# Four of the first layer's six input chunks multiplied as two Strassen units, with chained weight sums

## The chip, the cores and the metric

The kernel runs on one core of one Trainium2 chip. The metric is device time in microseconds (us) for one execution of the whole program. The kernel before takes 2197.44 us, the median of 3 runs (2197.28 to 2199.9).

## The reference, cut to what matters

Two transformer-like layers work on x of 256 rows (tokens) by 2048 columns, in float32. The first layer, with the parts that the change touches:

```
h  = x @ ev_w_in                      # 256x2048 @ 2048x3072
za = gelu(h[:, :2048]); xb = h[:, 2048:]
u, v = split(za)                      # 1024 columns each
v  = layer_norm(v, g, b)
ya = u * (tril(w_s) @ v per head + b_s)        # "gate": mixes rows, 8 heads of 128
yb = (pooling of xb over windows 2,4,8,16) @ w_pool * scale
mix = concat(ya, yb) @ ev_w_out       # 256x2048 @ 2048x2048
x  = layer_norm(ALPHA*x + mix)
x  = layer_norm(ALPHA*x + conv_ffn(x))         # w_up 2048x11264, w_down 5632x2048
```

The second layer has a gated recurrent mixer (w_in 2048x8192, w_out 2048x2048) in place of the gate and the pooling, and a conv_ffn of its own.

## The kernel before, in words

Nearly all of the work is products of x (256 rows, two halves t0 and t1 of 128) with weights. A weight matrix is cut into tiles of 512 rows by 512 columns (1 MiB). Four such tiles on top of each other make a chunk of 512 output columns. A float32 product is made of three passes: each weight tile is split by ScalarE into a rounded part wh (line 178) and by VectorE into the remainder wl (line 181), x likewise into xh and xl, and TensorE adds up xh*wh + xh*wl + xl*wh. One weight tile is therefore 4 (slices of 128 rows) x 3 (passes) x 2 (row halves) = 24 matmuls of 128 columns by 512.

The class Weights runs this stream. `_load` lists the tiles to fetch, `_feed` lists the tiles to split, in the order of use. `take` hands out the next split tile; before that it splits up to two tiles ahead, and `more` issues the loads for which a buffer is free (three raw buffers for ordinary tiles of kind 0; one buffer per tag for those of kind 1). Loads are issued by SyncE. `std` lists ordinary tiles. `chain` lists a Strassen unit: two chunks of columns by seven block products. A Strassen product needs half of the matmuls of an ordinary tile (12: one row half alone), so the unit has 7 x 12 for the upper two tiles of both chunks, and 4 x 24 for the lower two. Three of its products use sums of weight tiles. These are built in two raw buffers a and b: a is loaded, a second tile is added to it by an accumulating transfer that GpSimd issues (line 110, `then`); after a's first use a third tile is added, and after a difference on VectorE (line 113) a fourth. `strassen` (line 399) runs the products on TensorE in the order of UNIT_R[0] (P1, P7, s, P3, s, P6, P2, P5, s, P4, s; s is an ordinary tile); `snap` (line 424) copies a product from its accumulator bank, and VectorE joins them. `combine` (line 373) builds the four sums of x blocks that the products need. The second layer's mixer uses all of this already; the first layer before the change does not: its six input chunks (columns 2, 3 for v, 4, 5 for xb, 0, 1 for u) all go through `chunk` (line 330), 4 tiles of 24 matmuls each.

Around the chunks: after chunk 2 the function `loads0` issues the constants on SyncE (the norm's g and b, w_s, biases, scale, identity, pooling bands, 2.5 MB in all), after chunk 3 v is normalized. `later(n, fn)` keeps a piece of work back until TensorE has been given n more tiles' worth of work (`tick`); the gate, the pooling and the transposes of u are given to it. In the kernel before, the gate runs inside chunk 5 and the pooling inside chunk 0. x itself (two halves of 1 MiB) is loaded on SyncE after chunk 3 into x_t and first read at the end of `out_proj`'s first chunk. The program is handed to a scheduler that orders each engine's instructions by their place in the program and by when it expects them to be ready; semaphores are set by it.

Of the kernel before, what the change touches and what calls it, by code (L numbers as in the profile page):

```python
# [9 lines left out]
F32 = mybir.dt.float32  # L10
# [8 lines left out]
P = 128  # L19
# [16 lines left out]
class Weights:  # L36
# [3 lines left out]
    def __init__(self, nc, raw, hl, ahead):  # L40
# [10 lines left out]

        self.extra = {}


    def _load(self, ap, tag):
        r = {"ap": ap, "tag": tag, "last": None, "tile": None, "then": None, "phase": self.phase}
        self.loads[tag != "w"].append(r)
        return r

# [38 lines left out]
                if ap is not None:  # L98
                    self.std([ap])

    def chain(self, aps, rest, others=()):


        nc = self.nc
        a, b = self._load(aps[3], "qa"), self._load(aps[2], "qb")
        unit = UNIT_R[len(others)]
        rest, others = iter(rest), iter(others)

        def add(ap):
            nc.gpsimd.dma_start(a["tile"].rearrange("p k n -> p (k n)"), ap, accum_op=ALU.add)  # L110

        def t1():
            nc.vector.tensor_tensor(out=b["tile"], in0=a["tile"], in1=b["tile"], op=ALU.subtract)
            add(aps[1])

        a["then"] = lambda: add(aps[2])
        products = {"P7": (a, (), None, lambda: add(aps[0])), "P3": (b,), "P6": (a, (b,), None, t1),
                    "P5": (b,), "P4": (a,)}
        plain = {"P1": aps[0], "P2": aps[1]}
        for f in unit:  # L120
            if f in products:
                self._feed(*products[f])
            else:
                ap = plain[f] if f in plain else next(rest if f == "s" else others, None)
                if ap is not None:
                    self.std([ap])


    def load(self, pieces=1, between=None, kind=0):
        r = self.loads[kind][self.n_load[kind]]  # L130
        tag = r["tag"]
        r["tile"] = w = self.raw[kind].tile([P, 4, 512], F32, name=f"w{kind}_{self.n_load[kind]}", tag=tag)
        n = 4 // pieces
        for k in range(0, 4, n):
            if between is not None:
                between(k)
            self.nc.sync.dma_start(w[:, k:k + n].rearrange("p k n -> p (k n)"),
                                   r["ap"][:, k * 512:(k + n) * 512])
        if r["then"]:
            r["then"]()  # L140
        self.ring.setdefault(tag, []).append(r)
        self.n_load[kind] += 1
# [60 lines left out]
def block_kernel(ctx: ExitStack, tc: tile.TileContext, a, out):  # L203
# [14 lines left out]
    aux = ctx.enter_context(tc.tile_pool(name="aux", bufs=4, space=PSUM))  # L218

    W = Weights(nc, raw, hl, 2)  # L220
    for c in (2, 3, 4, 5, 0, 1):
        W.std([a["w_ev_in"][c, g] for g in range(4)])
    for c in range(4):
        W.std([a["w_ev_out"][c, g] for g in (2, 3, 0, 1)])

# [44 lines left out]
    def new_T(kind, g, pool=acts):  # L270
        h = pool.tile([P, 4, S], F32R, name=f"{kind}h{g}", tag=f"{kind}h{g}")
        l = pool.tile([P, 4, S], F32R, name=f"{kind}l{g}", tag=f"{kind}l{g}")
        return h, l
# [13 lines left out]
    with tc.tile_pool(name="xload", bufs=2) as xl:  # L287
# [18 lines left out]
        for g in (2, 3):  # L306
            split(XT[g], xr[g], np.s_[:, :, :])
            W.cast(4)
    x_t = [resid.tile([P, D], F32, name=f"x{t}", tag=f"x{t}") for t in range(2)]


    waiting = []
# [197 lines left out]
    def normalize(dst, src, mean, rs, g, b):  # L510
        V.scalar_tensor_tensor(out=dst, in0=src, scalar=mean, in1=g, op0=ALU.subtract, op1=ALU.mult)  # L511
        V.scalar_tensor_tensor(out=dst, in0=dst, scalar=rs, in1=b, op0=ALU.mult, op1=ALU.add)  # L512
# [8 lines left out]
    def load_gb(g_ap, b_ap, n=D, eng=G):  # L521
        g = gbp.tile([P, D], F32, name="g", tag="g")
        b = gbp.tile([P, D], F32, name="b", tag="b")
        eng.dma_start(g[:, 0:n], g_ap.rearrange("(o n) -> o n", o=1).broadcast_to([P, n]))
        eng.dma_start(b[:, 0:n], b_ap.rearrange("(o n) -> o n", o=1).broadcast_to([P, n]))
        return g, b
# [135 lines left out]

    ymix = ExitStack()
    yp = ymix.enter_context(tc.tile_pool(name="ymix0", bufs=1))
    YT = [new_T("y", g, yp) for g in range(4)]
    with tc.tile_pool(name="work0", bufs=1) as wk:
        v_t = [wk.tile([P, 1024], F32, name=f"v{t}") for t in range(2)]
        b_t = [wk.tile([P, 1024], F32, name=f"xb{t}") for t in range(2)]
        ws = wk.tile([P, 8, P], F32, name="ws")
        bs = wk.tile([P, 8], F32, name="bs")  # L670
        psc = wk.tile([P, 8], F32, name="psc")
        band = wk.tile([P, 4, 384], F32, name="band")

        def loads0():
            gb = load_gb(a["ln_v_g"], a["ln_v_b"], 1024, nc.sync)
            nc.sync.dma_start(ws, a["w_sT"].rearrange("p (h t) -> p h t", h=8))
            nc.sync.dma_start(bs, a["b_sT"])
            nc.sync.dma_start(psc, a["pool_scT"])
            nc.sync.dma_start(cst, a["cst"][:, 0:384].rearrange("p (k n) -> p k n", k=3))
            nc.sync.dma_start(band, a["cst"][:, 512:2048].rearrange("p (w n) -> p w n", w=4))  # L680
            for h in range(8):
                G.affine_select(ws[:, h], ws[:, h], pattern=[[1, P]], compare_op=ALU.is_ge, fill=0.0,
                                base=0, channel_multiplier=-1)
            return gb

        stv = [wk.tile([P, 2, 6], F32, name=f"stv{t}") for t in range(2)]

        def after_v(c):
            def f(t, ps):
                vs = v_t[t][:, c * 512:(c + 1) * 512]  # L690
                A.activation(vs, ps, AF.Gelu_apprx_tanh)
                V.bn_stats(stv[t][:, c], vs)
                if c == 1:
                    mean, rs = moments(stv[t])
                    normalize(v_t[t], v_t[t], mean, rs, gv[:, 0:1024], bv[:, 0:1024])
            return f

        def gate(t):
            for q in range(2):
# [4 lines left out]
                for k in range(4):  # L704
                    h = 4 * q + k
                    A.activation(v_t[t][:, h * P:(h + 1) * P], pg[:, k], AF.Identity, bias=bs[:, h:h + 1])

        def after_b(c):
            def f(t, ps):
                A.activation(b_t[t][:, c * 512:(c + 1) * 512], ps, AF.Copy)  # L710
            return f

        def pool(gi):
            wp = wk.tile([P, 2, S], F32, name="wp", bufs=2)
# [13 lines left out]
                kb = (gi % 2) * 2 + d  # L728
                split(YT[2 + gi // 2], py[:, d], np.s_[:, kb, :], scale=psc[:, gi * 2 + d:gi * 2 + d + 1])

        def after_u(c):
            def f(t, ps):
                u = wk.tile([P, 512], F32, name="u", bufs=2)
                A.activation(u, ps, AF.Gelu_apprx_tanh)
                V.tensor_tensor(out=u, in0=u, in1=v_t[t][:, c * 512:(c + 1) * 512], op=ALU.mult)
                later(1, lambda: transpose_split(YT[c], u, t))
            return f

        chunk(XT, 4, after_v(0))
        gv, bv = loads0()  # L740
        chunk(XT, 4, after_v(1))
        lower_bound()
        for t in range(2):
            nc.sync.dma_start(x_t[t], a["x"][t * P:(t + 1) * P])
        chunk(XT, 4, after_b(0))
        later(1, lambda: gate(0))
        later(2, lambda: gate(1))
        chunk(XT, 4, after_b(1))
        for gi in range(4):
            later(1 + gi, lambda gi=gi: pool(gi))  # L750
        chunk(XT, 4, after_u(0))
        chunk(XT, 4, after_u(1))
        XT = out_proj([YT[g] for g in (2, 3, 0, 1)], 4, True, a["ln1_g"][0], a["ln1_b"][0])
    ymix.close()


# [356 lines left out]
```

## Time and profile before

| | us |
|---|---|
| median of 3 runs | 2197.44 |
| the profiled execution | 2202.97 |
| its span (first to last instruction) | 2201.2 |
| TensorE busy in it | 2157.1 (98%) |
| VectorE busy | 1767.4 (80%) |
| ScalarE busy | 1230.3 (56%) |
| DMA moved | 489.00 MB, mean 222 GB/s |

A row of the timeline has start, duration, engine, source line, operation and tiles. Matmuls overlap, so a matmul's own duration (0.39 us) is longer than the step from one to the next. "idle before" and an arrow tell how long the engine stood still and what released it. Windows give busy time by engine, the granted TensorE clock, the DMA engines' busy share and their rate. In the profile "w<-in_w_ev_in" is the load of a first-layer input tile, "POOLq" a transfer issued by GpSimd.

### The profile page before, as it was taken

The numbers are of one execution on the slowest core, as the hardware profiler recorded it, in microseconds if no ns is written. First come the engines' busy times: TensorE is split into PE (matmuls) and PEld (weight loads), VectorE is DVE, ScalarE is ACT, GpSimd is POOL, SyncE is SP. The second block draws the span as 40 slices with busy tenths as digits, with TensorE's granted clock in tenths as the row PEclk, the third lists the DMA queues.
The fourth block names the chain that finished last, engine by engine and source line by source line (L and its number), as shares of the span: only waits on it lengthen the run. The fifth ranks groups of instructions, "written<-read, shape, count | busy, mean of one in ns | idle before, by whom it ended". The sixth has DMA issues, their size and how long they took to land. (4 is left out here: it accounts for less than half of the span.)

```text
span 2201.2 us, 24814 instructions
## 1 busy us (share of the span) xinstructions
PE 2157.1 (98%) x9887; PEld 1779.9 (81%) x9887; DVE 1767.4 (80%) x1706; ACT 1230.3 (56%) x1150; POOL 125.8 (6%) x140
## 2 busy tenths in 40 slices
PE   9999999999999999989999999999999999999997
PEld 7888788888888888878778888778888888888886
DVE  5545888888888888897687887888888888888888
ACT  5443455555655555646575756636555655555662
POOL 1000200000000000020000000030000000000000
PEclk9999999999999999999999999999999999999999
DMA  8646476777667677537778687746777666677743
GB/s 324 268 151 234 152 243 222 236 247 239 215 217 226 219 241 248 184 128 259 222 236 252 220 256 229 232 173 204 234 243 238 218 223 213 227 241 240 242 150 141
DMA packets 71796, 489.00 MB, mean 222 GB/s; under 512 B 8465, under 2 KB 9121, under 8 KB 13953
## 3 DMA queue, kind: packets, MB, share of 16 engines
q1 hardware_dynamic: 60656, 411.56, 50.0%
q0 software_dynamic: 11024, 75.86, 17.1%
q8 instruction: 77, 1.26, 0.2%
q14 instruction: 39, 0.31, 0.0%
HBM read 443.34 MB, written 2.11 MB: 202 GB/s over the span
## 5 line engine op out<-in xcount | busy, mean ns | idle before, releaser
L181 DVE TENSOR_TENSOR wl<-w,wh 128x2048 fp32r<-128x2048 f32 (+1 forms) x471 | 1051.2, 2235 | 337.7 <-ACT wh L178 334.2
L178 ACT ACTIVATE wh<-w 128x2048 fp32r<-128x2048 f32 (+1 forms) x495 | 894.7, 1813 | 628.7 <-PE pd L566 262.2
L412 PE MATMUL ps<-wh,xh 128*128 128x512 f32 x1188 | 468.0, 394 | 0.0
L412 PE MATMUL ps<-wl,xh 128*128 128x512 f32 x1188 | 462.8, 390 | 1.1 <-DVE wl L181 1.1
L412 PE MATMUL ps<-wh,xl 128*128 128x512 f32 x1188 | 462.8, 390 | 0.0
L566 PE MATMUL pd<-wh,yh 128*128 128x512 f32 x736 | 287.2, 390 | 3.2 <-DVE x L574 3.2
L566 PE MATMUL pd<-wl,yh 128*128 128x512 f32 x736 | 286.5, 389 | 0.4 <-DVE wl L181 0.4
L566 PE MATMUL pd<-wh,yl 128*128 128x512 f32 x736 | 286.4, 390 | 0.5 <-DVE yl L280 0.4
L412 PEld LDWEIGHTS ps<-wh,xl 128*128 128x128 f32 x1188 | 223.0, 188 | 46.7
L412 PEld LDWEIGHTS ps<-wl,xh 128*128 128x128 f32 x1188 | 223.3, 188 | 46.2 <-DVE wl L181 1.9
L412 PEld LDWEIGHTS ps<-wh,xh 128*128 128x128 f32 x1188 | 223.1, 188 | 45.0 <-ACT wh L178 0.4
L412 PE MATMUL ps<-wh,sh 128*128 128x512 f32 x432 | 169.8, 393 | 0.8 <-ACT u L424 0.5
L412 PE MATMUL ps<-wl,sh 128*128 128x512 f32 x432 | 168.9, 391 | 1.1 <-DVE wl L181 1.1
L412 PE MATMUL ps<-wh,sl 128*128 128x512 f32 x432 | 168.7, 390 | 0.0
L566 PEld LDWEIGHTS pd<-wh,yh 128*128 128x128 f32 x736 | 138.2, 188 | 32.5 <-DVE x L574 4.0
L566 PEld LDWEIGHTS pd<-wh,yl 128*128 128x128 f32 x736 | 138.1, 188 | 30.3 <-DVE yl L280 1.6
L566 PEld LDWEIGHTS pd<-wl,yh 128*128 128x128 f32 x736 | 138.2, 188 | 29.3 <-DVE wl L181 0.8
L341 PE MATMUL ps<-wh,xh 128*128 128x512 f32 x384 | 151.8, 397 | 1.6 <-ACT wh L178 1.6
L341 PE MATMUL ps<-wl,xh 128*128 128x512 f32 x384 | 151.2, 394 | 0.3 <-DVE wl L181 0.3
L341 PE MATMUL ps<-wh,xl 128*128 128x512 f32 x384 | 150.8, 393 | 0.0
L789 DVE SCALAR_TENSOR_TENSOR hc<-ph,cw,hc 128x254 f32<-128x254 f32 (+1 forms) x352 | 145.8, 475 | 1.4 <-ACT hc L786 1.2
L786 ACT ACTIVATE hc<-ph,cw 128x256 f32<-128x256 f32 x176 | 89.1, 556 | 62.5 <-DVE hc L789 58.8
(223 smaller groups left out, 2216.5 us busy)
## 6 DMA issues: line engine op xcount, KB each, us to landing
w<-in_w_up SPq DMA_DIRECT2D x176, 1024.0 KB, 4.9
w<-in_w_down SPq DMA_DIRECT2D x88, 1024.0 KB, 4.9
w<-in_w_od_in SPq DMA_DIRECT2D x64, 1024.0 KB, 6.6
w<-w POOLq DMA_DIRECT2D x40, 1024.0 KB, 8.1
w<-in_w_od_in POOLq DMA_DIRECT2D x21, 1024.0 KB, 9.2
w<-in_w_ev_in SPq DMA_DIRECT2D x20, 1024.0 KB, 5.2
w<-in_w_ev_out SPq DMA_DIRECT2D x16, 1024.0 KB, 4.8
w<-in_w_od_out SPq DMA_DIRECT2D x16, 1024.0 KB, 7.2
```

Of the source, the lines that this page charges most:

```text
L178: self.nc.scalar.activation(h[:, sl], w[:, sl], AF.Copy)
L181: eng.tensor_tensor(out=l[:, sl], in0=w[:, sl], in1=h[:, sl].bitcast(F32), op=ALU.subtract)
L341: T.matmul(ps[t], s[:, k, ts], m[:, k], start=(gi == 0 and k == 0 and i == 0), stop=(gi == n - 1 and k == 3 and i == 2))
L412: T.matmul(bank_, x[:, k, ts], m[:, k], start=(id(bank_) not in started), stop=(k == 3 and i == 2), skip_group_check=True)
L566: T.matmul(ps, x[:, k, t * P:(t + 1) * P], m[:, k], start=(k == 0 and i == 0), stop=(k == 3 and i == 2))
L786: A.activation(ob, pt[:, k], AF.Identity, scale=cw[:, 2, blk:blk + 1], bias=cw[:, 3, blk:blk + 1])
L789: V.scalar_tensor_tensor(out=ob[:, s:S], in0=pt[:, k, 0:S - s], scalar=cw[:, w, blk:blk + 1], in1=ob[:, s:S], op0=ALU.mult, op1=ALU.add)
```

## The change

Chunks 4, 5 and chunks 0, 1 become two Strassen units. The x sums are built with `combine` between chunk 2 and chunk 3, in the two buffers g and b that held the norm's scale and shift (these move to a tile of the pool ymix0). The chain's buffers qa and qb lie in the same pool, in the space of YT (the transposed gate and pooling results), which is now allocated when a unit is done with them. The second unit's buffer a is the tile x_t[0], so x is loaded only after the second unit. `W.open += 1; W.more()` stands ahead of `loads0`: it issues at once every load of kind 1 whose buffer is free. The gate is now given to `later` ahead of the first unit, the pooling ahead of the second; gelu on u reads the unit's results in x_t[1].

```diff
--- before.py
+++ after.py
@@ -51,9 +51,11 @@
 
         self.extra = {}
 
+        self.home = {}
+
 
     def _load(self, ap, tag):
-        r = {"ap": ap, "tag": tag, "last": None, "tile": None, "then": None, "phase": self.phase}
+        r = {"ap": ap, "tag": tag, "last": None, "tile": self.home.get(tag), "then": None, "phase": self.phase}
         self.loads[tag != "w"].append(r)
         return r
 
@@ -98,11 +100,11 @@
                 if ap is not None:
                     self.std([ap])
 
-    def chain(self, aps, rest, others=()):
+    def chain(self, aps, rest, others=(), tag="qa"):
 
 
         nc = self.nc
-        a, b = self._load(aps[3], "qa"), self._load(aps[2], "qb")
+        a, b = self._load(aps[3], tag), self._load(aps[2], "qb")
         unit = UNIT_R[len(others)]
         rest, others = iter(rest), iter(others)
 
@@ -129,7 +131,9 @@
     def load(self, pieces=1, between=None, kind=0):
         r = self.loads[kind][self.n_load[kind]]
         tag = r["tag"]
-        r["tile"] = w = self.raw[kind].tile([P, 4, 512], F32, name=f"w{kind}_{self.n_load[kind]}", tag=tag)
+        if r["tile"] is None:
+            r["tile"] = self.raw[kind].tile([P, 4, 512], F32, name=f"w{kind}_{self.n_load[kind]}", tag=tag)
+        w = r["tile"]
         n = 4 // pieces
         for k in range(0, 4, n):
             if between is not None:
@@ -218,8 +222,15 @@
     aux = ctx.enter_context(tc.tile_pool(name="aux", bufs=4, space=PSUM))
 
     W = Weights(nc, raw, hl, 2)
-    for c in (2, 3, 4, 5, 0, 1):
-        W.std([a["w_ev_in"][c, g] for g in range(4)])
+    x_t = [resid.tile([P, D], F32, name=f"x{t}", tag=f"x{t}") for t in range(2)]
+    W.home["x0"] = x_t[0].rearrange("p (k n) -> p k n", k=4)
+    we = a["w_ev_in"]
+    for c in (2, 3):
+        W.std([we[c, g] for g in range(4)])
+    W.phase += 1
+    for c in (4, 0):
+        W.chain([we[c, 0], we[c, 1], we[c + 1, 1], we[c + 1, 0]],
+                [we[c, 2], we[c, 3], we[c + 1, 2], we[c + 1, 3]], tag="x0" if c == 0 else "qa")
     for c in range(4):
         W.std([a["w_ev_out"][c, g] for g in (2, 3, 0, 1)])
 
@@ -306,7 +317,6 @@
         for g in (2, 3):
             split(XT[g], xr[g], np.s_[:, :, :])
             W.cast(4)
-    x_t = [resid.tile([P, D], F32, name=f"x{t}", tag=f"x{t}") for t in range(2)]
 
 
     waiting = []
@@ -662,17 +672,25 @@
 
     ymix = ExitStack()
     yp = ymix.enter_context(tc.tile_pool(name="ymix0", bufs=1))
-    YT = [new_T("y", g, yp) for g in range(4)]
+    raw[1] = yp
+    YT = {}
+
+    def new_Y(g):
+
+        y = yp.tile([P, 2, 4, S], F32R, name=f"y{g}", tag=("qa", "qb", "qc", "qd")[g])
+        YT[g] = (y[:, 0], y[:, 1])
+
     with tc.tile_pool(name="work0", bufs=1) as wk:
         v_t = [wk.tile([P, 1024], F32, name=f"v{t}") for t in range(2)]
-        b_t = [wk.tile([P, 1024], F32, name=f"xb{t}") for t in range(2)]
         ws = wk.tile([P, 8, P], F32, name="ws")
         bs = wk.tile([P, 8], F32, name="bs")
         psc = wk.tile([P, 8], F32, name="psc")
         band = wk.tile([P, 4, 384], F32, name="band")
 
         def loads0():
-            gb = load_gb(a["ln_v_g"], a["ln_v_b"], 1024, nc.sync)
+            gb = yp.tile([P, 2, 1024], F32, name="gbv", tag="qc")
+            for i, ap in enumerate((a["ln_v_g"], a["ln_v_b"])):
+                nc.sync.dma_start(gb[:, i], ap.rearrange("(o n) -> o n", o=1).broadcast_to([P, 1024]))
             nc.sync.dma_start(ws, a["w_sT"].rearrange("p (h t) -> p h t", h=8))
             nc.sync.dma_start(bs, a["b_sT"])
             nc.sync.dma_start(psc, a["pool_scT"])
@@ -681,7 +699,7 @@
             for h in range(8):
                 G.affine_select(ws[:, h], ws[:, h], pattern=[[1, P]], compare_op=ALU.is_ge, fill=0.0,
                                 base=0, channel_multiplier=-1)
-            return gb
+            return gb[:, 0], gb[:, 1]
 
         stv = [wk.tile([P, 2, 6], F32, name=f"stv{t}") for t in range(2)]
 
@@ -692,7 +710,7 @@
                 V.bn_stats(stv[t][:, c], vs)
                 if c == 1:
                     mean, rs = moments(stv[t])
-                    normalize(v_t[t], v_t[t], mean, rs, gv[:, 0:1024], bv[:, 0:1024])
+                    normalize(v_t[t], v_t[t], mean, rs, gv, bv)
             return f
 
         def gate(t):
@@ -704,11 +722,6 @@
                 for k in range(4):
                     h = 4 * q + k
                     A.activation(v_t[t][:, h * P:(h + 1) * P], pg[:, k], AF.Identity, bias=bs[:, h:h + 1])
-
-        def after_b(c):
-            def f(t, ps):
-                A.activation(b_t[t][:, c * 512:(c + 1) * 512], ps, AF.Copy)
-            return f
 
         def pool(gi):
             wp = wk.tile([P, 2, S], F32, name="wp", bufs=2)
@@ -728,29 +741,51 @@
                 kb = (gi % 2) * 2 + d
                 split(YT[2 + gi // 2], py[:, d], np.s_[:, kb, :], scale=psc[:, gi * 2 + d:gi * 2 + d + 1])
 
-        def after_u(c):
-            def f(t, ps):
+        def done_u(c, tiles):
+            if c == 0:
+
+                new_Y(0)
+                new_Y(1)
+            for t in range(2):
                 u = wk.tile([P, 512], F32, name="u", bufs=2)
-                A.activation(u, ps, AF.Gelu_apprx_tanh)
+                A.activation(u, tiles[t], AF.Gelu_apprx_tanh)
                 V.tensor_tensor(out=u, in0=u, in1=v_t[t][:, c * 512:(c + 1) * 512], op=ALU.mult)
-                later(1, lambda: transpose_split(YT[c], u, t))
-            return f
+
+                later(0.5, lambda t=t, u=u: transpose_split(YT[c], u, t))
+
 
         chunk(XT, 4, after_v(0))
+        W.open += 1
+        W.more()
         gv, bv = loads0()
+        tmp = [wk.tile([P, 2, 4, P], F32, name=f"cmb{t}", tag=f"xb{t}") for t in range(2)]
+        XS = combine(XT, *(v[:, i] for v in tmp for i in range(2)))
         chunk(XT, 4, after_v(1))
+        b_t = [wk.tile([P, 1024], F32, name=f"xb{t}", tag=f"xb{t}") for t in range(2)]
         lower_bound()
+
+
+        def tile_b(name, tag=None):
+            t, c = {"p1": (0, 0), "u3": (1, 0), "z": (0, 1), "c22": (1, 1), "p17": (0, None)}[name]
+            return x_t[1][:, 0:512] if c is None else b_t[t][:, c * 512:(c + 1) * 512]
+
+        def tile_u(name, tag=None):
+            i = ("p1", "u3", "z", "c22", "p17").index(name)
+            return x_t[1][:, i * 512:(i + 1) * 512] if i < 4 else spare[:, 0:512]
+
+        later(1, lambda: gate(0))
+        later(2, lambda: gate(1))
+        strassen(XT, XS, tile_b, lambda c, tiles: None, (), UNIT_R[0])
+        new_Y(2)
+        new_Y(3)
+        spare = yp.tile([P, 4 * 512], F32, name="spare", tag="qa")
+        for gi in range(4):
+            later(1 + gi, lambda gi=gi: pool(gi))
+        strassen(XT, XS, tile_u, done_u, (), UNIT_R[0])
         for t in range(2):
             nc.sync.dma_start(x_t[t], a["x"][t * P:(t + 1) * P])
-        chunk(XT, 4, after_b(0))
-        later(1, lambda: gate(0))
-        later(2, lambda: gate(1))
-        chunk(XT, 4, after_b(1))
-        for gi in range(4):
-            later(1 + gi, lambda gi=gi: pool(gi))
-        chunk(XT, 4, after_u(0))
-        chunk(XT, 4, after_u(1))
         XT = out_proj([YT[g] for g in (2, 3, 0, 1)], 4, True, a["ln1_g"][0], a["ln1_b"][0])
+    del raw[1]
     ymix.close()
 
 
```

## Rows read from the trace of the kernel before

**Rows 1.** The profile's page: busy time of the engines, granted clock in 40 slices.
```profile
PE 2157.1 (98%) x9887; PEld 1779.9 (81%) x9887; DVE 1767.4 (80%) x1706; ACT 1230.3 (56%) x1150; POOL 125.8 (6%) x140
PEclk9999999999999999999999999999999999999999
```

**Rows 2.** Waits of TensorE from 0 to 260 us: total us, times, longest.
```profile
PE pt L493 <- DVE x L512: 4.6, 3, 2.7
PE ps L341 <- ACT wh L178: 1.6, 2, 1.4
```

**Rows 3.** Timeline of TensorE in chunk 3: two matmuls, 24 steps apart.
```profile
49.70 0.39 PE L341 MATMUL ps<-wh,xl 128*128 128x512 f32 x1
...
55.14 0.39 PE L341 MATMUL ps<-wh,xl 128*128 128x512 f32 x1
```

**Rows 4.** Timeline of SyncE: loads issued around the constants.
```profile
35.84 0.33 SPq L137 DMA_DIRECT2D w<-in_w_ev_in  x1
36.22 0.42 SPq L524 DMA_DIRECT2D g<-in_ln_v_g  x1
...
39.36 0.47 SPq L680 DMA_DIRECT2D band<-in_cst  x1
40.72 16.28 SPq L137 DMA_DIRECT2D w<-in_w_ev_in  x4
```

**Rows 5.** Windows: busy us (count) of PE, PEld, DVE, ACT, POOL; clock; DMA share; GB/s.
```profile
8.00:28.00 20.00, 18.97 (x80) 14.69 (x81) 15.01 (x21) 15.45 (x22) 0.00 (x0) 1.00 1.03 407
36.00:54.60 18.60, 18.60 (x84) 15.40 (x83) 9.01 (x8) 6.96 (x6) 3.91 (x9) 1.00 0.94 360
```

**Rows 6.** DMA from 1026 to 1034 us: queue, packets, MB, share (one accumulating transfer).
```profile
q0 software_dynamic: 141, 1.05, 72.5%
```

**Rows 7.** Timelines of GpSimd: when the first-layer and chained transfers are issued.
```profile
64.52 0.60 POOL L524 DMA_DIRECT2D g<-in_ln_g  x1
...
1026.31 0.85 POOL L110 DMA_DIRECT2D w<-in_w_od_in  x1 [17.88 <-DVE wl L181]
```

**Rows 8.** DMA from 66 to 68 us, then from 68 to 73 us, by queue.
```profile
q1 hardware_dynamic: 108, 0.86, 101.5%
...
q0 software_dynamic: 258, 1.98, 95.3%
q1 hardware_dynamic: 28, 0.10, 4.8%
```

**Rows 9.** Timelines of ScalarE and VectorE: one tile's split, chunk 3's end, v's normalization.
```profile
41.96 1.92 ACT L178 ACTIVATE wh<-w 128x2048 fp32r<-128x2048 f32 x1 [3.52 <-PE ps L341]
...
53.78 0.59 ACT L691 ACTIVATE v<-ps 128x512 f32<-128x512 f32 x1
...
43.91 2.29 DVE L181 TENSOR_TENSOR wl<-w,wh 128x2048 fp32r<-128x2048 f32 x1 [3.14 <-ACT wh L178]
...
56.55 1.28 DVE L512 SCALAR_TENSOR_TENSOR v<-v,rs,b 128x1024 f32<-128x1024 f32 x1
```

**Rows 10.** Timeline of TensorE and ScalarE: the gate; P1 to P7 in the second layer.
```profile
80.47 1.95 PE L703 MATMUL pg<-v,ws 128*128 128x128 f32 x16
82.17 0.48 PE L341 MATMUL ps<-wh,xh 128*128 128x512 f32 x1
...
1027.53 0.39 PE L412 MATMUL ps<-wh,xl 128*128 128x512 f32 x1
1027.93 0.73 PE L412 MATMUL ps<-wh,xh 128*128 128x512 f32 x2
1027.95 0.60 ACT L424 ACTIVATE p<-ps 128x512 f32<-128x512 f32 x1
1028.61 0.51 PE L412 MATMUL ps<-wh,sh 128*128 128x512 f32 x1
```

**Rows 11.** Windows after a wait of TensorE in the second layer: granted clock third from last.
```profile
976.00:980.00 4.00, 2.09 (x10) 1.58 (x10) 3.29 (x7) 0.72 (x1) 2.07 (x5) 0.89 0.68 243
980.00:984.00 4.00, 4.00 (x17) 3.09 (x16) 2.39 (x5) 1.20 (x2) 0.00 (x0) 0.69 0.21 85
984.00:988.00 4.00, 4.00 (x23) 3.23 (x21) 4.00 (x7) 2.22 (x2) 0.00 (x0) 1.00 0.00 0
```

**Rows 12.** Windows of the later chunks and of the start of the output projection.
```profile
53.60:99.60 46.00, 45.68 (x219) 38.13 (x218) 26.71 (x25) 23.35 (x32) 3.90 (x4) 1.00 0.71 284
158.00:180.00 22.00, 22.00 (x102) 18.30 (x102) 11.77 (x9) 8.92 (x7) 0.55 (x1) 1.00 0.75 293
```

## The prediction

> **What bounds the kernel now.** I read the page first: TensorE is busy for 98% of the span at full granted clock, VectorE for 80% [rows 1]. So only time taken off TensorE's own stream, or waits put into it, can show. Next the waits of TensorE over the first 260 us: behind the start-up waits for the first tiles (1.6 us) there are only the 4.6 us at the end of the layer, where the normalized x is transposed [rows 2]. Between about 15 and 240 us the stream has no wait worth naming, so matmuls removed there are worth their full step. The step is read from the timeline of chunk 3: 24 matmuls, one weight tile, take 55.14 - 49.70 = 5.44 us, or 0.227 us each [rows 3]. Then I looked at what feeds it at that time, SyncE's issues and the DMA engines: from 36.0 to 54.6 us they are at 0.94 of their time [rows 4, 5]. This is the resource with least to spare where the change adds most.
>
> **What is removed.** A unit has 7 x 12 + 4 x 24 = 180 matmuls, the two chunks it replaces have 8 x 24 = 192. Two units: 24 matmuls x 0.227 = **5.4 us** off TensorE. Gate, pooling and transposes keep their matmuls and only move.
>
> **What is added on VectorE and ScalarE.** A unit has 11 tiles to split where two chunks have 8: 3 x 2.29 = 6.9 us of VectorE [rows 9]; the difference of two raw tiles, as long as a split, 2.3; five joins of 512 columns at about 0.7 (estimated from v's 1.28 for 1024 columns [rows 9]), 3.5. Together 12.7 us. In 53.6 to 99.6 VectorE is busy for 26.7 of 46 us [rows 12], so 39 of some 44 in the first unit: tight, but lying beside TensorE. If that cover fails, it is the products P6, P2, P5 in a row (8.2 us for 2.3 + 3 x 2.29 = 9.2 us of splitting) that wait, 1 us a unit; I take 0. The x sums (12 operations of 0.7, 8 us) fall into chunk 3, where VectorE has 9.0 of 18.6 us busy [rows 5]: 0, up to 1 if they delay a split. Between P1 and P7 both products use one bank, so P7 waits for the copy. The second layer shows it: last matmul of P1 at 1027.53, two matmuls of the next tile slipped in, P7 at 1028.61 [rows 10]: 1.08 - 3 x 0.227 = **0.4 us a unit, 0.8 in all**.
>
> **The queue ahead of P7.** Up to 36 us nothing of the change is issued. Then `W.more()` puts three loads of 1 MiB on SyncE ahead of the constants, not one: the first unit's a and b, and also the second unit's a, since its home x_t[0] is free and both chains are of one phase. Two accumulating transfers follow on GpSimd, each when its a has landed, both ahead of the mask on w_s in GpSimd's order.
>
> Prices: a plain MiB takes 1.049 MB / 407 GB/s = 2.6 us of all engines [rows 5]. An accumulated one took 72.5% of 8 us = 5.8 us [rows 6]. The window that ends at 54.6 us has 0.94 x 18.6 = 17.5 us of work, which began therefore at 37.1; it moved 6.70 MB, four weight tiles (8 to 11) and 2.5 MB of constants; less 4 x 2.6 the constants took 7.2 us [rows 5].
>
> In the changed order: tile 8 until 39.7, first a 42.3, b 44.8, second a 47.4, constants 54.6. The constants are issued within 3.6 us [rows 4], so by about 41.2, before the first accumulation can be (a landed at about 43, and 0.85 us to issue [rows 7]). What order the engines keep between the two queues is shown at 64.5 us: a GpSimd transfer issued there got nothing until the older SyncE transfers were through (66 to 68 us: SyncE's queue alone, 101.5%), then had the engines for itself [rows 7, 8]. So the first accumulation runs from 54.6 to 60.4 and is seen at about 61.4. ScalarE's copy takes 1.92 and VectorE's remainder 2.29 [rows 9]: P7's first matmul at 63.3, its second at 65.7. TensorE is there earlier: gelu on the last product of chunk 3 starts at 53.78 [rows 9], so P1 runs from 53.5 to 56.2 and P7 is due at 56.6 (second matmul 56.8). That is **8.9 us late**; 2.6 more if tile 10's load gets in ahead of it.
>
> Not all of it need be idle. The first gate (1.7 us, 80.47 to 82.17 [rows 10]) wants v normalized, in the kernel before at 57.8 [rows 9], and P3 (12 matmuls, 2.7 us) wants b alone, which landed long ago. The two matmuls slipped in ahead of P7 in the second layer [rows 10] show that TensorE's order is not bound to the program's. I count both as cover, **-4.4 us**; it is 0 if the scheduler does not see the delay, and it is the softest term.
>
> A wait of such length has brought the clock down: after the waits at 976 to 980 us the granted clock was 0.89 and then 0.69 in two windows of 4 us, that is 0.9 + 2.5 = 3.4 us at the lower level, 1.2 GHz [rows 11], losing half of it, 1.7. I take half of this, **0.8 us**.
>
> Behind P7, tile 10 has landed by about 57 to 64 and is not late again; the third accumulation (after P7's split) has P3 and 24 to 48 matmuls of cover, 8 to 14 us for 5.8.
>
> **The end of the layer.** x (2 MiB, 5.2 us) is loaded after the second unit, and the output norm's scale and shift (as much again) can start only when the x sums are dead; both are wanted 20 us or more later. At 158 to 180 us the DMA engines are busy for 0.75 [rows 12], which leaves 5.5 us, and earlier more. Nothing, or up to 3 us if SyncE stands at x's load with tiles of `ev_w_out` behind it. Gelu reads SBUF instead of the bank, and its transposes come two half tiles later; the output projection has two tiles (10.9 us) to do before it needs them: 0, at most 1.
>
> **The sum** against the profiled execution (2202.97 us, span 2201.2): -5.4 + 0.8 + 8.9 - 4.4 + 0.8 = +0.7 us, 2203.7. That execution lies 5.5 us above the median of the runs; on the median's scale the forecast is 2198.1, rounded to **2198 us**. A change under 0.2%, 4.4 us, is what a measurement of this kernel can hardly tell from none.
>
> **Rival 1: no wait.** If the loads of a and b get to the engines before 36 us (the buffers are free from 22 us on) or the accumulation is served as soon as issued (44 to 50 us), P7's tile is in time and tile 10 as well. Then -5.4 + 0.8 = -4.6: 2192.8. Against it: SyncE keeps the program's order there, with each constant right behind the load of tile 8 though its buffer was free all along [rows 4].
>
> **Rival 2: the second sum in front of tile 10, slower.** If the two queues share the engines, the first sum comes in time, and the ordinary tile behind P7 pays: before it the engines must do tiles 8 and 10, three loads, constants and one accumulation, 5.2 + 7.8 + 7.2 + 5.8 = 26 us from 37.1; seen at 64.1 and split at 68.3, where TensorE wants it at 61.2 (P7 and a gate done). That is 7.1 us, and 12.9 if the second accumulation is in front too; about 10. With the clock's 1.7 and little to slip in: -5.4 + 0.8 + 10 + 1.7 = +7.1: 2204.5. The same comes out if queues keep their order but TensorE's does not bend. It decides from the point where the wait is over 9 us.
> The Trainium skill ("DMA: Bandwidth & Descriptors", Queues, rings and completion order) states that a DMA engine goes round-robin between the rings it has work for, a packet at a time. By that rule this rival would be the one; the trace at 66 to 68 us does not bear it out [rows 8].
>
> **Rival 3: not what it says.** "First chained sum ahead" also brings the second's; if x_t[0]'s load or its accumulation sits on the constants, v's normalization (wanted at 53, VectorE in order) holds up the splits behind it: 2 to 5 us more on the forecast, 2200 to 2203.
>
> **Chances.** Forecast 0.42 (own range 2194 to 2203), rival 1 0.26, rival 2 0.24, rival 3 0.08. Faster by over 0.2%: most of rival 1 (0.19) and the forecast's lower end (0.07), 0.26. Slower: rival 2 (0.22), the forecast's upper end (0.07), part of rival 3 (0.03), 0.32. Within: 0.42. The range from rival 1 to a little over rival 2: 2191.5 to 2206.
>
> **What would show it.** TensorE's waits between 53 and 75 us: a gap of 3 to 9 us ahead of the first matmuls with xsums (line 412, wh and sh) released by the split means P7's sum was late; ahead of the ordinary tile behind it, rival 2; none, rival 1. The accumulation's issue at about 44 us and its landing, the time of P3 and of the gate in TensorE's order, and the granted clock right after the gap show the other terms. It is wrong altogether if TensorE's gain is given back elsewhere: at P6 for VectorE, or at the output projection's first x.

## The result: 0.74% slower

| | before | after |
|---|---|---|
| median, us (runs) | 2198.67 (4) | 2216.18 (4) |
| lowest to highest | 2197.28 to 2202.91 | 2215.61 to 2218.84 |
| profiled execution (span) | 2202.97 (2201.2) | 2215.68 (2214.0) |

The ratio after/before is 1.0074, with a 95% interval of 1.0056 to 1.0092: 17.5 us, between 12.3 and 20.2. That is outside the range of the prediction.

The page of the changed kernel has 24 TensorE matmuls less than [rows 1], as planned. GpSimd's queue takes 18.4% of the DMA engines' span.

```profile
PE 2155.3 (97%) x9863; PEld 1776.3 (80%) x9863; DVE 1797.9 (81%) x1736; ACT 1246.8 (56%) x1166; POOL 130.0 (6%) x146
q0 software_dynamic: 11888, 82.16, 18.4%
```

The loss lies in the first layer. Its last step, the first transposes of the normalized x, starts 15.7 us later than in the kernel before (241.57 there). The timeline of TensorE has that row:

```profile
257.25 0.63 PE L503 MATMUL pt<-cst,x 128*128 128x128 f32 x4
```

TensorE's longest waits from 0 to 260 us (total us, times, longest), to be laid beside [rows 2]; those at the end of the layer, 4.6 us there, fall for the most part behind 260 us here:

```profile
PE ps L422 <- ACT wh L182: 11.5, 2, 10.9
PE ps L422 <- ACT xb L434: 3.3, 1, 3.3
PE ps L422 <- DVE wl L185: 0.4, 1, 0.4
```

L422 is the matmul of the Strassen units. The two large waits are one behind the other in the first unit, as the timeline of TensorE shows:

```profile
56.37 0.39 PE L422 MATMUL ps<-wh,xl 128*128 128x512 f32 x1
60.07 0.50 PE L422 MATMUL ps<-wh,sh 128*128 128x512 f32 x1 [3.30 <-ACT xb L434]
...
64.91 0.40 PE L422 MATMUL ps<-wh,sl 128*128 128x512 f32 x1
76.21 1.22 PE L422 MATMUL ps<-wh,xh 128*128 128x512 f32 x2 [10.90 <-ACT wh L182]
```

P1 ends at 56.4, P7 (tiles wh and sh) runs from 60.07 to 65, and the ordinary tile behind P7, tile 10, starts at 76.21. ScalarE's timeline says what each waited for:

```profile
56.64 1.91 ACT L182 ACTIVATE wh<-w 128x2048 fp32r<-128x2048 f32 x1 [11.53 <-PE ps L422]
58.46 1.07 ACT L709 ACTIVATE v<-ps 128x512 f32<-128x512 f32 x2
59.41 0.60 ACT L434 ACTIVATE xb<-ps 128x512 f32<-128x512 f32 x1
...
74.25 5.51 ACT L182 ACTIVATE wh<-w 128x2048 fp32r<-128x2048 f32 x3 [8.31 <-DMA w<-in_w_ev_in]
```

The first sum was there at 56.6; its copy, two gelu's of v and the copy of P1's bank stand in a row on ScalarE, and P7 needs the last. Tile 10's data came only at 74.2. SyncE had issued that load at 48.76, behind the unit's loads and all the constants:

```profile
36.13 1.28 SPq L141 DMA_DIRECT2D w<-in_w_ev_in  x3
37.45 0.69 SPq L141 DMA_DIRECT2D x<-in_w_ev_in  x1
...
40.87 0.33 SPq L696 DMA_DIRECT2D psc<-in_pool_scT  x1
43.34 0.33 SPq L697 DMA_DIRECT2D cst<-in_cst  x1
45.83 0.33 SPq L698 DMA_DIRECT2D band<-in_cst  x1
48.76 11.70 SPq L141 DMA_DIRECT2D w<-in_w_ev_in  x3
```

The last three constants and tile 10's load each had to wait. SyncE's waits from 40 to 49 us (total us, times, longest) name the landing of a load:

```profile
SPq L141 <- DMA x<-in_w_ev_in: 2.5, 1, 2.5
SPq L698 <- DMA w<-in_w_ev_in: 2.1, 1, 2.1
SPq L697 <- DMA w<-in_w_ev_in: 2.1, 1, 2.1
SPq L696 <- DMA w<-in_w_ev_in: 0.6, 1, 0.6
```

Each time it is the load issued eight places earlier: tile 8 (36.13), a, b and the second unit's a (37.45). So at most eight of SyncE's transfers were under way here.

GpSimd issued three accumulations in that time, at 44.10, 48.99 and 61.17:

```profile
44.10 0.92 POOL L112 DMA_DIRECT2D w<-in_w_ev_in  x1 [41.12 <-DMA w<-in_w_ev_in]
48.99 0.85 POOL L112 DMA_DIRECT2D x<-in_w_ev_in  x1 [3.97 <-DMA x<-in_w_ev_in]
61.17 0.84 POOL L112 DMA_DIRECT2D w<-in_w_ev_in  x1 [11.34 <-DVE wl L185]
```

The DMA queues from 44 to 49 us, and then from 50 to 55 (packets, MB, share of the engines; q0 is GpSimd's, q1 SyncE's):

```profile
q1 hardware_dynamic: 270, 1.72, 95.3%
q0 software_dynamic: 2, 0.02, 1.7%
...
q0 software_dynamic: 102, 0.84, 80.3%
q1 hardware_dynamic: 102, 0.35, 19.4%
```

For nearly 5 us after its issue the first accumulation gets nothing; then both queues get the same number of packets. What this leaves to SyncE depends on the size of its packets. From 50 to 55 us they are the constants' (0.35 MB in 102, 3.4 KB in the mean, against 8.2 KB), and SyncE has a fifth of the engines. From 66 to 71 us its packets are as large as the accumulation's; it has over a third then, and a packet of the accumulation takes twice as long as one of a load (68.3/87 against 35.9/90):

```profile
q0 software_dynamic: 87, 0.71, 68.3%
q1 hardware_dynamic: 90, 0.72, 35.9%
```

The queue ahead of tile 10 is thus, with the prices of the prediction: from 37.1, two tiles 5.2, three loads 7.8, constants 7.2 and three accumulations 17.4, together 37.6 us: 74.7. Its copy began at 74.25. That the two are so close is in part luck. The queues from 37.1 to 74.2 us:

```profile
q1 hardware_dynamic: 1823, 8.59, 59.6%
q0 software_dynamic: 432, 3.15, 41.2%
```

The accumulations took 41.2% of 37.1 us, 15.3 and not 17.4 (5.1 each). SyncE's queue took 22.1 where the sum has 20.2, for it moved 8.59 MB, 0.8 MB more than the five loads and the constants.

TensorE's granted clock is low behind both waits. Windows from 61.3 us on (busy us and count of PE, PEld, DVE, ACT, POOL; granted clock; DMA share; GB/s):

```profile
61.30:64.70 3.40, 3.40 (x10) 2.66 (x9) 3.26 (x8) 0.00 (x0) 2.10 (x6) 0.50 1.03 382
64.70:68.10 3.40, 0.61 (x3) 0.17 (x1) 1.43 (x2) 0.60 (x1) 3.18 (x6) 1.00 1.05 307
68.10:76.20 8.10, 0.00 (x0) 0.00 (x0) 0.01 (x1) 1.95 (x2) 0.00 (x0) 0.50 1.01 344
76.20:81.70 5.50, 4.91 (x11) 3.27 (x12) 5.50 (x4) 3.56 (x2) 0.00 (x0) 0.50 0.62 200
81.70:86.00 4.30, 4.30 (x20) 3.58 (x19) 4.30 (x6) 0.66 (x1) 0.00 (x0) 0.99 0.23 95
...
82.00:257.00 175.00, 175.00 (x805) 145.07 (x803) 109.11 (x90) 85.26 (x83) 7.05 (x10) 1.00 0.65 222
```

It is at 1.2 GHz while P7 runs and again while tile 10's first matmuls run, 3.4 and 4.9 us of work, half of which is lost: 4.2. From 82 us to the layer's end TensorE is busy throughout; nothing is lost there.

The balance up to the layer's end: 1.2 that the start-up took longer (tile 8's copy at 43.20, 41.96 in [rows 9]), waits 3.3 + 0.4 + 10.9 + 0.6 (the last at 78.0, for the next tile's copy) = 15.2, clock 4.2, less the 5.4 removed: +15.2 against the 15.7 measured. The spans differ by only 12.8 us; the kernel before lost some time in the second layer to stretches of half clock, as in [rows 11] (its granted clock from 1200 to 1500 us is 0.98, the changed kernel's 1.00).

### The profile page after: what moved, and what is told of

Read it like the earlier page. It is cut to its first block, busy times and chain, and to the rows that moved or that the text cites. A ratio compares the mean times of both kernels' runs of the same rounds, so it can differ in the third digit from the quotient of the medians.

```text
span 2214.0 us, 24841 instructions
## 1 busy us (share of the span) xinstructions
PE 2155.3 (97%) x9863; PEld 1776.3 (80%) x9863; DVE 1797.9 (81%) x1736; ACT 1246.8 (56%) x1166; POOL 130.0 (6%) x146
## 3 DMA queue, kind: packets, MB, share of 16 engines
q0 software_dynamic: 11888, 82.16, 18.4%
## 5 line engine op out<-in xcount | busy, mean ns | idle before, releaser
L422 PE MATMUL ps<-wh,xh 128*128 128x512 f32 x1276 | 504.4, 396 | 10.9 <-ACT wh L182 10.9
L422 PE MATMUL ps<-wl,xh 128*128 128x512 f32 x1276 | 498.7, 391 | 3.1 <-DVE wl L185 3.1
L422 PE MATMUL ps<-wh,xl 128*128 128x512 f32 x1276 | 498.7, 391 | 0.0
L422 PEld LDWEIGHTS ps<-wh,xh 128*128 128x128 f32 x1276 | 240.4, 189 | 59.8 <-ACT wh L182 11.5
L422 PEld LDWEIGHTS ps<-wl,xh 128*128 128x128 f32 x1276 | 240.6, 189 | 52.4 <-DVE wl L185 4.7
L422 PEld LDWEIGHTS ps<-wh,xl 128*128 128x128 f32 x1276 | 240.2, 188 | 50.5
L422 PE MATMUL ps<-wh,sh 128*128 128x512 f32 x464 | 183.2, 395 | 4.5 <-ACT xb L434 3.3
L422 PE MATMUL ps<-wl,sh 128*128 128x512 f32 x464 | 181.2, 391 | 0.4 <-DVE wl L185 0.4
L422 PE MATMUL ps<-wh,sl 128*128 128x512 f32 x464 | 181.4, 391 | 0.0
L584 DVE TENSOR_TENSOR x<-x,pd 128x512 f32<-128x512 f32 x160 | 105.8, 683 | 5.3 <-PE pd L576 1.7
L422 PEld LDWEIGHTS ps<-wh,sh 128*128 128x128 f32 x464 | 87.6, 189 | 24.4 <-ACT xb L434 3.7
L351 PE MATMUL ps<-wh,xh 128*128 128x512 f32 x256 | 102.0, 401 | 1.3 <-ACT wh L182 1.3
```

The source lines that it names most:

```text
L351: T.matmul(ps[t], s[:, k, ts], m[:, k], start=(gi == 0 and k == 0 and i == 0), stop=(gi == n - 1 and k == 3 and i == 2))
L422: T.matmul(bank_, x[:, k, ts], m[:, k], start=(id(bank_) not in started), stop=(k == 3 and i == 2), skip_group_check=True)
L584: V.tensor_tensor(out=xs, in0=xs, in1=ps, op=ALU.add)
```

## The experiments

Theory A: the loss is volume, whatever goes to the DMA engines ahead of tile 10's load or beside it, accumulations above all. Rivals: B, that the order "ahead of the constants" does the harm; C, that the accumulations alone do; D, that a large part is the clock; E, that something of the unit itself (the order of work on ScalarE and VectorE, P7's sum) is at fault. The recorded expectations use the letters from B on in senses of their own, which each explains; A is the same throughout. "Layer end" below is the start of the first `pt<-cst,x` transpose in the profile: 241.6 before, 257.2 after. "Longest wait" is TensorE's from 16 to 100 us. The three groups were timed against 31, 26 and 18 runs of the kernel before (medians 2202.83, 2202.20 and 2201.18); these runs scatter from 2192 to 2212, so ratios are known to some 0.15%. Against these medians the changed kernel's 2216.18 would be 1.0061 to 1.0068, a little less than in its own comparison.

**The second chain held back** until the first unit is under way:

```diff
-    W.phase += 1
     for c in (4, 0):
+        W.phase += 1
...
+        later(3, lambda: setattr(W, "open", W.open + 1))
         strassen(XT, XS, tile_b, lambda c, tiles: None, (), UNIT_R[0])
```

> The second unit's chain is opened only in the middle of the first unit; all else as in the changed kernel. Theory A (the DMA engines are short of time ahead of tile 10, and the GpSimd accumulations share them with the loads): one load (2.6 us) and one accumulation (5.8 us) less stand ahead of tile 10, so the 11 us wait of TensorE ahead of the first ordinary tile of the unit falls to 2 to 4 us and the run takes about 2206 to 2208. Theory B (the order on ScalarE: the split of P7's tile ahead of gelu and of P1's copy is what delays all behind it): that order is the same, so the time stays at 2214 to 2217. Theory C (a unit's extra work on VectorE and ScalarE is too much for the first layer): no change, 2214 to 2217.

**No accumulations** (`if self.no_sum: return` ahead of line 112):

> The six accumulating transfers of the first layer are left out (its weight sums are therefore not formed); loads, splits and products stay. Theory A: 17.4 us of DMA time less ahead of tile 10, no wait at P7 nor at tile 10, so 24 matmuls less and two bank waits more: 4 to 5 us under the kernel before, 2192 to 2196. Theory B: the 3 us wait ahead of P7 goes, the 11 us stays if it is not the DMA: about 2212. Theory C: nothing changes on VectorE and ScalarE, 2212 to 2216.

**Plain copies in their place**, the same bytes by the same queue (`accum_op=ALU.add` dropped):

> The six transfers of the first layer on GpSimd stay, with the same bytes from the same places, but as plain copies instead of accumulations (the sums are therefore not formed). Theory A by volume: each takes 2.6 instead of 5.8 us of DMA time, 9.6 us less ahead of tile 10, so the 11 us wait falls to 1 to 3 us: 2204 to 2208. If it is the number of GpSimd transfers or their waits that cost (theory B): 2212 to 2217. Theory C: 2214 to 2217.

**The first chain's loads earlier**, on top of the first experiment, in chunk 2; the constants stay:

```diff
+        later(2, lambda: setattr(W, "open", W.open + 1))
         chunk(XT, 4, after_v(0))
-        W.open += 1
-        W.more()
```

> As the run with the second chain held back, and the first chain's two loads and its first accumulation are issued in the middle of chunk 2, ahead of tiles 7 and 8, in the stretch around 28 to 36 us where the DMA engines stand idle. Theory A: the two loads and one accumulation, 11 us, use idle time; P7's sum is in time and only the constants and perhaps one accumulation are ahead of tile 10: no wait over 1 us, 2193 to 2197. Theory B: P7's tile no longer holds up ScalarE, so the 3 us go, the 11 us stay: about 2212. Theory C: 2213 to 2217.

| | ratio to before (95%) | layer end | longest wait, us |
|---|---|---|---|
| second chain held | 1.0026 (1.0014 to 1.0038) | 248.3 | 4.0 |
| no accumulations | 1.0013 (1.0000 to 1.0026) | 244.4 | 2.5 |
| plain copies | 1.0020 (1.0007 to 1.0032) | 248.0 | 6.5 |
| first chain earlier | 0.9997 (0.9981 to 1.0013) | 242.3 | 1.6 |

TensorE's waits from 16 to 100 us in the first and the third of these, and then the DMA queues of the third from 50 to 55 us:

```profile
PE ps L422 <- DVE wl L185: 4.3, 2, 4.0
PE ps L422 <- ACT xb L434: 3.0, 1, 3.0
```

```profile
PE ps L426 <- ACT wh L186: 7.1, 2, 6.5
```

```profile
q0 software_dynamic: 168, 1.25, 60.1%
q1 hardware_dynamic: 215, 0.75, 39.4%
```

Holding back the second chain, a load of 1 MiB and an accumulation, takes the wait ahead of tile 10 from 10.9 to 4.0 us and brings 8.9 us back at the layer's end; P7's wait stays (3.0). I had expected 2 to 4 us, but the 4.0 left are not what I meant: tile 10 was there at 60.3 instead of 74.2, in time. VectorE came to its remainder only at 66.43, since v's normalization had slid behind P7's late tile and kept it busy from 59.6 on (ScalarE, then VectorE):

```profile
60.32 3.71 ACT L182 ACTIVATE wh<-w 128x2048 fp32r<-128x2048 f32 x2 [1.52 <-DVE stv L710]
...
66.43 4.49 DVE L185 TENSOR_TENSOR wl<-w,wh 128x2048 fp32r<-128x2048 f32 x2
```

Without any accumulation TensorE still waits 3.4 us in two waits, where I expected none, and the granted clock is 0.58 and 0.54 from 62.3 to 70 us. But tile 10 is not late: its load, issued at 48.37, landed 9.6 us later, at 58.0, while P7 ran to 59.9. ScalarE stood idle until then, since the copy of P7's bank stands ahead of tile 10's copy in its order:

```profile
59.90 0.60 ACT L437 ACTIVATE x<-ps 128x512 f32<-128x512 f32 x1 [3.10 <-PE ps L425]
60.39 5.50 ACT L185 ACTIVATE wh<-w 128x2048 fp32r<-128x2048 f32 x3
```

So this run does not speak against C. The plain copies do: with nothing added, tile 10's load, issued at 48.56, took 16.7 us to land, and TensorE waits 6.5 us for it where I expected 1 to 3. Beside the loads the copies take 60% of the engines and move 1.25 MB in 5 us, so GpSimd's transfers compete for the engines even when they add nothing.

With the first chain's loads early enough that its accumulation is issued at 35.4 instead of 44.1 us, all of the loss comes back: no measurable difference from the kernel before. (The DMA engines were not idle from 28 to 36 us, as the expectation has it, but at 0.61 and 0.73 of their time in the changed kernel.) The unit's own work (E) is thus not the loss. But no gain from the 24 matmuls less shows either: the layer ends at 242.3 against 241.6. TensorE still waits 0.7 us for the copy of P1's bank, 1.6 for a remainder from VectorE and 1.1 for the lower bound's transpose.

**The constants spread.** On top of the last: g and b of the norm stay in `loads0`, w_s, b_s and the identity go behind tile 10 (`later(1, loads1)`), the bands into the unit (`later(4, loads2)`), the x sums into chunk 3:

```diff
-        XS = combine(XT, *(v[:, i] for v in tmp for i in range(2)))
+        XS = []
+        later(0.5, lambda: XS.extend(combine(XT, *(v[:, i] for v in tmp for i in range(2)))))
+        later(1, loads1)
...
+        later(4, loads2)
```

> As the run with the first chain issued in chunk 2, and further: of the constants only the norm's scale and shift stay behind chunk 2; the mask's weights, biases and identity are issued behind tile 10, scale and bands in the middle of the first unit; the x sums are built one tile later. Theory A (volume on the DMA engines ahead of tile 10): 1.5 MB less ahead of tile 10, about 4.7 us, so the last 1.9 us of wait there go, and no half-clock stretch in the first unit: 1 to 3 us under the run with the early first chain, that is 0.999 to 0.9975 of the kernel before. Theory D (the start, where the x sums' copies delay the first splits): 1 us of this comes from a start with no extra wait before 16 us. If neither: the same as the early first chain, 0.9997.

**Constants first, chains behind them**, nothing else changed:

```diff
+        gv, bv = loads0()
         W.open += 1
         W.more()
-        gv, bv = loads0()
```

> One part of the change alone undone: the first chain's loads are issued behind the constants. Theory A: the work ahead of tile 10 is the same, so the waits of TensorE at P7 and at tile 10 together stay between 12 and 18 us, but their place moves to P7, whose sum comes 5 to 7 us later: 1.006 to 1.009 of the kernel before, as the changed kernel (1.0074). Theory E (the constants' lateness, through the norm of v and the mask, is the cost): the gate and v come 8 us earlier and the time falls to 1.000 to 1.003.

**1.5 MB of the constants behind tile 10's load**, else as changed (`later(1, lambda: (loads1(), loads2()))`):

> The changed kernel with mask weights, biases, scale, identity and bands (1.5 MB) issued behind tile 10's load; the chains and all accumulations as in it. Theory A: 4.7 us less ahead of tile 10, its copy begins at about 69 to 70 instead of 74.3 us, the wait falls from 11 to 6 us and part of the half-clock loss with it: 1.004 to 1.006 of the kernel before. Theory E: no gain or a loss, since these constants come later still: 1.007 to 1.010.

**Useless matmuls in the two waits**, 13 behind P1 and 44 behind P7 (`strassen(..., dummies=(13, 44))`), for the clock:

> The changed kernel with 13 matmuls without use between P1 and P7 (2.9 us) and 44 between P7 and the ordinary tile behind it (10.0 us), in TensorE's two waits. What they show is what the lower clock behind the waits costs: if it is the waits that bring the clock down, the 3.4 us and 13.7 us stretches at half clock go and the end of the first layer comes 3 to 4.5 us earlier: 1.005 to 1.006 of the kernel before. If the clock falls for another reason, or the stretches cost nothing: 1.007 to 1.008.

| | ratio to before (95%) | layer end | longest wait, us |
|---|---|---|---|
| constants spread | 0.9996 (0.9984 to 1.0009) | 240.8 | 1.6 |
| constants first | 1.0044 (1.0028 to 1.0059) | 253.6 | 9.9 |
| constants behind tile 10 | 1.0028 (1.0010 to 1.0047) | 251.5 | 4.0 |
| useless matmuls | 1.0068 (1.0046 to 1.0090) | 262.4 | 5.1 |

TensorE's waits from 16 to 100 us with the constants first, and with 1.5 MB of them behind tile 10:

```profile
PE ps L422 <- ACT wh L182: 9.9, 1, 9.9
```

```profile
PE ps L422 <- ACT wh L182: 4.1, 4, 1.2
PE ps L422 <- ACT xb L434: 4.0, 1, 4.0
```

Spreading the constants was to bring 1 to 3 us over the early first chain; 0.9996 against 0.9997 shows no gain, though the layer ends 1.6 us earlier. With the constants first the kernel is still slower than the one before; the one long wait is now ahead of P7 (56.2 to 66.1 us), whose sum comes later, and tile 10 is in time. The order mostly says which product pays for the volume, so B is not the cause. It may have a share: the layer ends 3.6 us earlier than in the changed kernel, the ratio is below what I expected, and its interval just touches the changed kernel's. Taking 1.5 MB of the constants out of the way instead leaves P7's 4.0 us and little of tile 10's wait (1.2, and 1.1 for the tile behind it), with a ratio again below the 1.004 that I expected at least. The useless matmuls settle nothing on D: the clock was full from 66 to 76 us but still at half from 62.1 to 65.5, and TensorE then waited 5.1 us for a transpose of the lower bound that stands right behind tile 10 in this run (behind P3 and the next tile in the changed kernel), after which the clock fell too:

```profile
66.00:76.00 10.00, 10.00 (x45) 8.09 (x44) 2.07 (x3) 3.87 (x3) 1.78 (x5) 1.00 1.02 320
...
86.00:92.00 6.00, 4.59 (x21) 4.50 (x22) 1.17 (x7) 2.04 (x8) 0.00 (x0) 0.50 0.33 134
```

What the clock costs is thus known only from the windows of the changed kernel, not by a run that took it away.

**The spread version with the lower bound moved** into the second unit, since VectorE was now busy for 24.2 of the 25 us from 54 to 79:

```diff
-        lower_bound()
...
+        later(5, lower_bound)
         strassen(XT, XS, tile_u, done_u, (), UNIT_R[0])
```

> As the run with the constants spread, and the second layer's lower bound (its transfer, nine small operations on VectorE, a table load and a transpose) moved from the first into the second unit. That run still waited 1.0 us ahead of this transpose, 1.0 us for a remainder and 1.7 us for a copy, with VectorE at work without a pause from 54 to 79 us. Theory F (once the DMA engines are in time, VectorE's extra 12.7 us per unit are the next bound): 2 us less on VectorE there takes 1 to 2.5 us of the 3.7 us away, the layer ends at 238 to 240 instead of 240.8 us, 0.9985 to 0.9995 of the kernel before. If these waits come from the order alone: they move, and the layer ends at 240 to 241.5, 0.9996.

**The volume alone, in the kernel before:** two loads of 1 MiB and three accumulations into x_t ahead of the constants, no unit:

```diff
+        for t in range(2):
+            nc.sync.dma_start(x_t[t], a["w_ev_out"][t, 0])
+            G.dma_start(x_t[t], a["w_ev_out"][2 + t, 0], accum_op=ALU.add)
+        G.dma_start(x_t[0], a["w_ev_out"][0, 1], accum_op=ALU.add)
```

> The kernel before, with no unit in the first layer, but with two plain loads of 1 MiB and three accumulating transfers put in ahead of the constants (into x_t, which the load of x overwrites later). Theory A: volume on the DMA engines alone brings the waits: 2 x 2.6 + 3 x 5.8 = 22.6 us in front of or beside tiles 9 and 10, of which the slack takes some 8 us: TensorE waits 10 to 16 us between 54 and 80 us, 1.005 to 1.008 of the kernel before. If it is the unit's own work (bank copies, splits, x sums) that made the wait: under 3 us, 1.000 to 1.001.

| | ratio to before (95%) | layer end | longest wait, us |
|---|---|---|---|
| spread, lower bound moved | 0.9988 (0.9970 to 1.0006) | 238.8 | 1.4 |
| volume alone | 1.0098 (1.0065 to 1.0131) | 262.4 | 17.4 |

TensorE's wait in the kernel with the volume alone (timeline), and a window of it; then its longest wait from 16 to 100 us in the version with the lower bound moved:

```profile
75.96 1.22 PE L341 MATMUL ps<-wh,xh 128*128 128x512 f32 x2 [17.44 <-ACT wh L178]
...
61.10:81.60 20.50, 4.54 (x10) 3.14 (x11) 5.66 (x4) 5.73 (x3) 0.56 (x1) 0.50 0.91 323
```

```profile
PE pg L725 <- DVE v L522: 1.4, 1, 1.4
```

The volume alone makes the kernel before wait 17.4 us, more than I expected, behind the same 24 matmuls and until the same time (75.96 here, 76.21 in the changed kernel), with no unit in it. This is theory A by itself. More than I had counted went ahead of the tile: GpSimd's plain load of the output norm's scale, 1 MiB, was issued at 60.05 and took 12.9 us to land. With it the volume is that of the changed kernel, three plain MiB, three accumulations and the constants. The last version is the best one: 2197.85 us against 2201.18, its profile's layer end 2.7 us before that of the kernel before. But its interval holds 1 (from -6.6 to +1.3 us), so it is not shown to be faster.

## Why the prediction was wrong, step by step

**The matmuls removed, -5.4: right.** 9863 instead of 9887, at the same step, and TensorE busy without a gap from 82 to 257 us.

**Two bank copies, +0.8: about right as a sum.** The second unit shows no wait for `xb`; in the first it is the end of a longer one, and 0.7 in the two runs in which the sum was in time (no accumulations, first chain earlier).

**P7's sum late, +8.9: the step that failed.** It rested on a reading of [rows 8]: a GpSimd transfer gets nothing until SyncE's older loads are through, then has the engines for itself. The first half is a late start (64.5 to 68 there, 44.1 to 49 here); the second I saw only because SyncE's loads ran out at that moment. The changed kernel, with loads still waiting, shows equal packets for both queues, 102 and 102. Nor were the constants issued by 41.2, as I had reckoned from [rows 4]: SyncE, held up by the three loads, issued the last at 45.83, behind the first accumulation. So the sum came at 56.6, not 61.4, P7 was 3.5 us late (60.07 where 56.6 was due), and the accumulations that I had put behind tile 10 went in front of it. The rule of the Trainium skill ("DMA: Bandwidth & Descriptors", Queues, rings and completion order), round-robin between rings a packet at a time, agrees with these numbers and with 87 and 90 from 66 to 71 us, though the profile does not tell whether its packets are those that the Trainium skill means; I had set the rule aside.

**Behind P7 nothing late: failed with it, and cost most.** The prediction had 0 here, the runs 11.5 us. This was rival 2, and its mechanism is what happened, with the wrong count. It had one accumulation in front of tile 10, two at most, and a wait of 7.1 to 12.9 us. Because the first sum came early, the third accumulation could be issued at 61.2, ahead of tile 10's landing too. With three in front the sum gives 74.7 us, and the trace has 74.25 (with terms that are off by 2 us each way, as said above). The wait was 10.9, not more, only because P7 itself had been late.

**Cover by P3 and the gate, -4.4: failed.** In the timeline P1, P7 and tile 10 follow one another with nothing between; the scheduler did not see the delay, the case for which the prediction had this term at 0. P3's tile could not have served: ScalarE copied it behind tile 10, in the row of three from 74.25 on. Nor could the gate: VectorE finished v's normalization at 80.9, behind tile 10's remainder.

**The clock, +0.8: too small.** Two spells, 4.2 us of lost work. Rival 2 had 1.7.

**VectorE and the end of the layer, 0: right** in the changed kernel, where the DMA waits hid any strain on VectorE in the first unit. Once they are gone it shows: 4.0 us with the second chain held, 1.6 with the first chain earlier, both for a remainder that stands behind v's normalization, and in the spread version TensorE's remaining waits there are for splits and the lower bound. For the first unit the 0 had no room to spare.

With the measured sizes the prediction's own sum is -5.4 + 3.7 (P7, with the 0.4 behind it) + 11.5 + 4.2 = +14.0, and +15.2 with the start-up's 1.2, which has nothing to do with the change's steps as far as the runs show.

## What to carry to other kernels

Count what must pass the DMA engines before the next ordinary tile lands, from both queues, the accumulations that become possible later included; removing 2.7 us of matmuls from a unit can pay only if the 1 MiB loads and the accumulations of 5 to 6 us that it brings lie where the engines have time. Here, 9 us earlier, they cost nothing that could be measured; that the change then gains is not shown. A wait that remains after such a move can be of another kind, as VectorE's 4.0 us were: look at when the tile landed before counting it. A row that shows one queue waiting for another shows an order only if the first still had work when the second began. An edit that opens one load may open every load of its phase: the second chain's share was 8.9 of the 15.7 us.

## What the runs showed of the hardware

- An accumulating transfer and SyncE's loads got packets in nearly equal number (102 and 102, 87 and 90). The shares of the engines followed the packets' cost: 80.3% to 19.4% beside constants of 3.4 KB a packet, 68.3% to 35.9% beside weight loads of 8 KB. Plain copies by the same queue took 60.1% beside the constants, with 168 packets to 215.
- An accumulated MiB took 5.1 us of the engines in the changed kernel (41.2% of 37.1 us for three), 5.8 in [rows 6].
- A GpSimd transfer started late when loads were queued: 3.5 us after its issue in [rows 8], nearly 5 in the changed kernel. Why was not tried.
- SyncE paused between the constants, 40.87, 43.34, 45.83 and 48.76 us, where in [rows 4] they left without a pause: each of these issues waited for the landing of the load eight places earlier, and the change had put three loads of 1 MiB among those.
- The granted clock was 0.50 from 61.3 us on, after a wait of 3.3 us.
